# Norm factors with a token to a partition, and gates ahead of attention's end, in a two-layer gated-branch trunk

## The chip, the cores and the metric

The kernel runs on one core of a Trainium2 chip. The metric is the device time of one execution in microseconds. A time is given as the median of several runs; the profile comes from one execution, with its own time.

## The reference, cut to what matters

Two layers of a trunk run over 640 tokens of width 1024: 128 context tokens and 512 latent tokens, with one set of weights. The two groups differ in their modulation vectors, in attention and in the scan's starting state.

```
mod = silu(cond) @ w_mod + b_mod;  shift, scale, gate = split(mod, 3)
h = rmsnorm(x, g_norm) * (1 + scale) + shift
(a_u, a_v, b_r, b_k, b_v, b_wd, b_ad, c_q, c_k, c_v, d_p, z, mg) = split(h @ w_in)
y_a = chunk_mix(a_u, a_v)      # a_u * (128x128 mix of a_v in each chunk + b_s)
y_b = rwkv7_mix(...)           # scan forward and backward, group norm, bonus
y_c = attention(c_q, c_k, c_v) # windows of 128, cached keys and values, sink
y_d = pool_mix(d_p)            # means over 2, 4, 8, 16 tokens minus the token, a small product
ys = stack(y_a, y_b, y_c, y_d) * silu(z)
merged = sum_n sigmoid(mg_n) * (ys_n @ w_up_n)
x = x + gate * (merged @ w_o)
```

After layer 2 a last RMSNorm gives the outputs. rmsnorm divides each token by the root of its mean square over the 1024 features; the factor is one number for each token. Keys, values and the context's last scan states are outputs too.

## The kernel before, in words

Activations lie with features on the partitions and tokens along the free axis: 1024 features are eight tiles (KT) of 128, and the 640 tokens are two halves (b = 0, 1) of HF = 320. Large products are made from three: both operands are split into a high and a low part (`hi`, `lo` for activations, `whi`, `wlo` for weights; ScalarE makes the high part, VectorE the low one), and hi-whi, lo-whi and hi-wlo are added in PSUM. A weight tile of w_in (one entry of ORDER, in two pieces of four blocks) needs 48 products with 320 columns for both halves. All matrix products are issued from line 331, transposes from 335, all work of VectorE, ScalarE and GpSimd from 290, and all loads and stores from 327 on SP's queue, so rows are told apart by their tiles.

PSUM has four banks `m` for these products, two `x` for side work, and one each of `c` and `o`.

The instruction order is made when the kernel is built, by a small planner (`Clock`). There is a main stream (`layer`), which goes through ORDER and the merges, and there are side jobs (modulation, norm, attention, scan, pooling, chunk mixing, modulation rows), each with a priority. A side job that is ready by the planner's estimate goes ahead of the main stream, which fills the rest. A `yield "name"` waits in the planner until that job is marked done; a bare `yield` gives others a turn; `VQ` asks that VectorE's queue be nearly empty. On the chip each engine works through its own instructions in the order that came out, and waits for its operands.

The places that the change touches:

- `rstd_of` makes the norm's factor. `nacc` holds sums of squares (128 feature rows x 320 tokens). A product with a constant matrix of 1/1024 sums over partitions and puts the mean of each token on all 128 partitions; ScalarE takes the square root and VectorE the reciprocal of all 128x320. It runs for both halves at the start (`program`), at the layers' border (`normed`, where the last square tile comes in as `more`) and at the end (`fin`).
- `modulation` makes layer 0's shift and scale: eight jobs, one for each feature tile, each with a load of 1 MB, a `partial` (eight products with `sc`), a copy (`vn`) and two small products with the constant `sel`. The norm's tile k waits for job k. `modulation_rows` makes the other modulation vectors on VectorE from 32 loads of `wt` and a broadcast silu of the conditions (`sil`), one dot product (`junk`) per row and group.
- `gated` multiplies a branch by silu(z): tanh on ScalarE, two multiplications on VectorE, then the split into `ysh` and `ysl`. For attention (z20, z21) it first makes both products, then waits for attention's end (`{L}at`), with both tiles held in the four `m` banks.
- `attention` goes through ten blocks of 128 queries: scores in two parts with masks and maxima on VectorE (tile `kbt`), exponentials on ScalarE, transposes, and the product with the values.
- `pool_mix` copies the product of p0 or p1 into a padded buffer in the tile xm1 and spawns the pooling job; `chunk_v` and `chunk_u` do the chunk mixing of the a branch in the tile xm0. Attention's tables lie in xm1 before, and the merge's sums `mg` take both tiles after.
- `merge` goes through eight feature tiles of a branch: 48 products for the gate mg, 12 for w_up.

The end of `layer`, which orders these:

```python
        g2 = yield from gated(None, f"{L}at")
        ...
        for ft in range(2):
            yield from pool_mix(ft, buf, yd)
            yield from chunk_v(ft, tm, bs, ya)
        yield from chunk_u(ya)
        for ft in range(2):
            yield f"{L}pool{ft}"
        yield from merge(0, g2, mhl)
```

## Time and profile before

| | |
|---|---|
| median of three runs | 1417.62 us (1411.64 to 1418.31) |
| the profiled execution | 1418.08 us, span 1416.0 us |
| TensorE matmul busy | 1358.9 us, 96% of the span |
| VectorE, ScalarE, GpSimd busy | 944.7, 566.8, 50.8 us |
| loaded and stored | 132.59 MB, 94 GB/s in the mean |
| mean granted TensorE clock | 0.991 |

Busy times of engines overlap, so they don't add up to the span. A busy TensorE isn't one at its peak, since matmuls are pipelined and their ends are modelled. PE is TensorE's products, PEld its weight loads, DVE VectorE, ACT ScalarE, POOL GpSimd, SPq SP's queue. A span is the time from the first to the last instruction; the execution's own time is some 2 us longer. The granted clock is a share of TensorE's upper level, 2.4 GHz; its other level is 1.2 GHz.

### The profile page before, as it was taken

How to read it: one execution, taken by the hardware profiler on the slowest of the kernel's cores; microseconds unless marked ns; L12 is line 12 of the kernel's file. 1: busy time of each engine (PE TensorE's matmuls, PEld its weight loads, DVE VectorE, ACT ScalarE, POOL GpSimd, SP SyncE). 2: the span in 40 equal slices, each digit the busy share in tenths (PEclk: the TensorE clock that was granted, in tenths of full speed). 3: DMA queues.
4: the chain of work that ended last, by engine and by line, in shares of the span. 5: the costliest groups of instructions: out<-in, count | busy, mean ns of one | idle time of the engine just before them, and what ended most of it. 6: DMA issues, size and time to landing. Idle time of an engine off the chain costs nothing.

```text
span 1416.0 us, 27587 instructions
## 1 busy us (share of the span) xinstructions
PE 1358.9 (96%) x11274; PEld 1256.8 (89%) x11274; DVE 944.7 (67%) x2096; ACT 566.8 (40%) x1252; POOL 50.8 (4%) x43
## 2 busy tenths in 40 slices
PE   6899988999999999999999999999999999999996
PEld 3788878988999988999988888998799999899996
DVE  6666677755876756656887677795466585464476
ACT  5446522235533233324454655223345233232363
POOL 0000010000000000000001000100000000000001
PEclk9999999999999999999999999999999999999998
DMA  9411214421224412562313111424122323144111
GB/s 369 147 53 61 63 40 120 105 82 56 88 65 112 119 55 75 196 234 62 105 61 112 54 46 39 121 79 118 42 59 69 90 81 89 37 128 173 28 38 75
DMA packets 86503, 132.59 MB, mean 94 GB/s; under 512 B 44745, under 2 KB 46153, under 8 KB 84457
## 3 DMA queue, kind: packets, MB, share of 16 engines
q1 hardware_dynamic: 86376, 130.84, 30.1%
q8 instruction: 88, 1.44, 0.4%
q14 instruction: 39, 0.31, 0.1%
HBM read 120.46 MB, written 10.35 MB: 92 GB/s over the span
## 4 chain that ended last, share of the span: by engine, by line
PE 81%; DVE 10%; ACT 4%; issue 2%; DMA 2%; SPq 0%; POOL 0%; DVEq 0%; ACTq 0%; POOLq 0%
PE m L331 63%; PE x L331 10%; PE c L331 4%; PE o L331 2%; DVE wlo L290 2%; DVE t L290 2%; DVE kb L290 2%; ACT whi L290 1%; DMA kb<-ad 1%; PE x L335 1%; DVE nacc L290 1%; PE o L335 1%; DVE lo L290 1%; ACT vn L290 1%; ACT A L290 1%
## 5 line engine op out<-in xcount | busy, mean ns | idle before, releaser
L331 PE MATMUL m<-hi,whi 128*128 128x320 f32 x2064 | 666.7, 323 | 2.9 <-ACT whi L290 1.3
L331 PE MATMUL m<-lo,whi 128*128 128x320 f32 x2064 | 640.8, 310 | 6.0 <-DVE lo L290 5.1
L331 PE MATMUL m<-hi,wlo 128*128 128x320 f32 x2064 | 642.1, 311 | 3.9 <-DVE wlo L290 3.8
L331 PEld LDWEIGHTS m<-hi,whi 128*128 128x128 f32 x2064 | 389.6, 189 | 27.6 <-issue 11.4
L331 PEld LDWEIGHTS m<-lo,whi 128*128 128x128 f32 x2064 | 390.1, 189 | 10.2 <-DVE lo L290 7.1
L331 PEld LDWEIGHTS m<-hi,wlo 128*128 128x128 f32 x2064 | 389.4, 189 | 8.5 <-DVE wlo L290 8.2
L290 ACT CAST whi<-raw 128x640 fp32r<-128x640 f32 (+1 forms) x220 | 148.7, 682 | 296.3 <-PE m L331 270.6
L290 DVE TENSOR_TENSOR wlo<-raw,whi 128x640 fp32r<-128x640 f32 (+1 forms) x220 | 169.2, 772 | 108.6 <-ACT whi L290 105.8
L290 ACT ACTIVATE t<-m 128x320 f32<-128x320 f32 x160 | 68.3, 437 | 88.2 <-PE m L331 88.0
L290 DVE SCALAR_TENSOR_TENSOR t<-t,m 128x320 f32<-128x320 f32 x128 | 61.6, 482 | 58.9 <-PE m L331 43.5
L290 DVE TENSOR_TENSOR kb<-kb 80x31 f32<-80x31 f32 (+15 forms) x248 | 86.1, 347 | 13.0 <-DMA kb<-ad 6.1
L331 PE MATMUL m<-ysh,whi 128*128 128x320 f32 x256 | 84.3, 329 | 1.8 <-DVE t L290 1.6
L290 DVE CUSTOM_DVE_ANT_0 junk<-wt,sil 128x1024 bf16<-128x1024 f32 x64 | 78.4, 1224 | 3.1 <-DMA wt<-wt 3.0
L331 PE MATMUL m<-ysl,whi 128*128 128x320 f32 x256 | 79.6, 311 | 0.0
L331 PE MATMUL m<-ysh,wlo 128*128 128x320 f32 x256 | 79.6, 311 | 0.0
L331 PEld LDWEIGHTS m<-ysh,whi 128*128 128x128 f32 x256 | 48.6, 190 | 5.1 <-DVE t L290 2.1
L290 DVE TENSOR_TENSOR xm<-xm,t 128x320 f32<-128x320 f32 x96 | 48.5, 506 | 3.3
L331 PEld LDWEIGHTS m<-ysl,whi 128*128 128x128 f32 x256 | 48.7, 190 | 0.4
L331 PEld LDWEIGHTS m<-ysh,wlo 128*128 128x128 f32 x256 | 48.6, 190 | 0.0
L290 DVE RECIPROCAL t<-t 128x320 f32<-128x320 f32 x16 | 34.4, 2150 | 19.5 <-ACT t L290 19.5
L290 ACT ACTIVATE vn<-c 64x128 f32<-64x128 f32 x40 | 10.8, 271 | 80.5 <-DVE vn L290 80.5
L290 DVE CUSTOM_DVE_ANT_0 kbt<-x,xm 128x256 f32<-128x256 f32 (+2 forms) x72 | 28.7, 435 | 16.2 <-PE x L331 16.0
(234 smaller groups left out, 1528.4 us busy)
## 6 DMA issues: line engine op xcount, KB each, us to landing
raw<-wb SPq DMA_DIRECT2D x128, 320.0 KB, 3.0
raw<-wa SPq DMA_DIRECT2D x92, 256.0 KB, 2.8
wt<-wt SPq DMA_DIRECT2D x32, 512.0 KB, 3.7
A<-wm SPq DMA_DIRECT2D x4, 1024.0 KB, 9.0
A<-wo SPq DMA_DIRECT2D x8, 512.0 KB, 4.0
xm<-xt SPq DMA_DIRECT2D x4, 640.0 KB
ad<-A SPq DMA_DIRECT2D x8, 320.0 KB, 4.3
qr<-wm SPq DMA_DIRECT2D x2, 1024.0 KB
```

The lines of the kernel that those rows point to most:

```text
L290: return f(out, *a, **k)
L331: PE.matmul(out, lhsT, rhs, start=start, stop=stop)
L335: PE.transpose(out, in_, K("ident"))
```

## The change

- The norm factors. `rstd_thin` puts a token on a partition: each 128 tokens of the sums of squares are the stationary operand, and two columns of the constant 1/1024 the moving one, so the means come out as 128x2 for each of three token blocks. Square root and reciprocal then run on 128x6. `spread` brings the factors back to all partitions: a column of factors, read 128 times over, is the stationary operand, and the identity is the moving one; a copy puts the result where `rs` is read. At the end VectorE reads the factors from PSUM, and GpSimd the copy.
- The start. The first modulation job's products are issued between the first half's means and its spreading, and the job's second part between the second half's.
- The modulation rows. The load of `sil` is issued when the eight jobs are done, its arithmetic 4 us later by the planner's clock; a row waits for VectorE at most six times.
- Attention. A block whose four key blocks fit one bank makes its scores in one part. `pt` is allocated ahead of `yc`.
- The gates. `gates_early` makes silu(z) up to a factor and keeps it in the tile `ysl`; then p0's product follows, and only then the wait for attention's end; `gates_late` multiplies by the branch and splits.
- Pooling. ORDER has p1 after av1; the pooling jobs are spawned before and after the two chunk_v, the loads of `pc` are issued after the late gates, and the wait for both pooling jobs moves into the merge, behind its first w_up products.

```diff
 PAIRS = (HEAD[0:2], HEAD[2:4])
-ORDER = ["wa", "k0", "v0", "r0", "k1", "r1", "v1", "z20", "z21", "p0", "av0", "p1", "av1", "au0", "au1", 0,
+ORDER = ["wa", "k0", "v0", "r0", "k1", "r1", "v1", "z20", "z21", "p0", "av0", "av1", "p1", "au0", "au1", 0,
          "z00", "z01", 1, "z30", "z31", 2, "z10", "z11", 3]
...
         yield
-        if arrival(0) > 0:
-            yield arrival(0)
         nx = partial(0)
...
             nx = None
-            if i + 1 < len(jobs) and arrival(i + 1) <= 0.05:
+            if i and i + 1 < len(jobs) and arrival(i + 1) <= 0.05:
                 nx = partial(i + 1)
...
         mod_tiles(1)
+        yield "mods0"
         sil = S([P, 2, D], "sil")
...
         w = S([P, D], "wt")
-        yield "mods0"
+        yield 4.0
         for g in range(2):
...
             for g in range(2):
-                while ck.free.get("V", 0.0) > ck.t + 0.3:
-                    yield VQ
+                for _ in range(6):
+                    if ck.free.get("V", 0.0) > ck.t + 0.3:
+                        yield VQ
                 V.tensor_tensor_reduce(junk, w, sil[:, g], 1.0, 0.0, ALU.mult, ALU.add,
...
-    def rstd_of(acc, more=None):
+    def rstd_thin(acc, more=None):
+
         ms = X()
-        mm(ms[:, 0:HF], K("mean"), acc, start=True, stop=more is None)
-        if more is not None:
-            mm(ms[:, 0:HF], K("mean"), more, start=False, stop=True)
-        A.activation(acc, ms[:, 0:HF], AF.Sqrt, bias=eps[:, 0:1])
-        V.reciprocal(acc, acc)
-        return acc
+        parts = [acc] if more is None else [acc, more]
+        for i, o in enumerate((0, P, HF - P)):
+            for x in parts:
+                mm(ms[:, 2 * i:2 * i + 2], x[:, o:o + P], K("mean")[:, 0:2], start=i == 0 and x is acc,
+                   stop=i == 2 and x is parts[-1])
+        st = S([P, 6], "rst", 2)
+        A.activation(st, ms[:, 0:6], AF.Sqrt, bias=eps[:, 0:1])
+        V.reciprocal(st, st)
+
+        def spread():
+            bc = X()
+            for i, (o, c) in enumerate(((0, 0), (P, 0), (2 * P, C))):
+                mm(bc[:, o:min(o + P, HF)], st[:, 2 * i:2 * i + 1].to_broadcast([P, P]), K("ident")[:, c:P])
+            A.copy(acc, bc[:, 0:HF])
+            return bc
+
+        return spread
...
         for b in bs:
-            rs[b] = accs[b] if l == 0 else rstd_of(accs[b], more)
+            rs[b] = accs[b]
+            if l:
+                rstd_thin(accs[b], more)()
         for b in bs:
...
-        def gated(y, need=None):
+        def gated(y):
             hi = S([P, 2, T], "ysh", dt=F32R)
             lo = S([P, 2, T], "ysl", dt=F32R)
-            zs = []
-            if need:
-                for ft in range(2):
-                    zs.append((yield from main()))
-                yield need
-                y = inputs["yc"]
             for ft in range(2):
-                z = zs[ft] if need else (yield from main())
+                z = yield from main()
                 for b in range(2):
...
+        def gates_early():
+
+            early = S([P, 2, T], "ysl")
+            for ft in range(2):
+                z = yield from main()
+                for b in range(2):
+                    t = early[:, ft, hs[b]]
+                    A.activation(t, z[b], AF.Tanh, scale=0.5)
+                    V.scalar_tensor_tensor(t, t, 1.0, z[b], ALU.add, ALU.mult)
+            return early
+
+        def gates_late(early, y):
+            ts = []
+            for ft in range(2):
+                for b in range(2):
+                    ts.append(S([P, HF], "t", 4))
+                    V.scalar_tensor_tensor(ts[-1], early[:, ft, hs[b]], 0.5, y[:, ft, hs[b]], ALU.mult, ALU.mult)
+            hi = S([P, 2, T], "ysh", dt=F32R)
+            lo = S([P, 2, T], "ysl", dt=F32R)
+            for i, t in enumerate(ts):
+                o = (slice(None), i // 2, hs[i % 2])
+                A.copy(hi[o], t)
+                V.tensor_tensor(lo[o], t, hi[o], ALU.subtract)
+            return hi, lo
+
         mg = []
...
         def merge(i, yhl, mhl):
-            if i == 0:
-                mg.extend(x_tile(b) for b in range(2))
             rhs_y = [((lambda k, b=b: yhl[0][:, k, hs[b]]), (lambda k, b=b: yhl[1][:, k, hs[b]])) for b in range(2)]
...
                 yield from accum(up, w, 3, 2, rhs_y, 0, True, True)
+                if i == 0 and dt == 0:
+                    for ft in range(2):
+                        yield f"{L}pool{ft}"
+                    mg.extend(x_tile(b) for b in range(2))
                 for b, g in enumerate(gs):
...
-        def pool_mix(ft, buf, yd):
+        def pool_mix(ft, buf, yd, o):
             pw = prm("pw").rearrange("p (f c) -> p f c", f=2)
-            o = yield from main()
-            if ft:
-                yield f"{L}pool0"
             xp, s2, s4 = (buf[:, i * W:(i + 1) * W] for i in range(3))
...
             yield f"{L}cv"
+            pt = S([P, 2 * T], "y", 2)
             yc = inputs["yc"] = S([P, 2, T], "y", 2)
-            pt = S([P, 2 * T], "y", 2)
             vt = inputs["cv"]
...
                     rs = [slice(0, 64), slice(64, 128)]
-                    px = [X(), X()]
-                    for hh, r in enumerate(rs):
-                        mm(px[hh][:, 0:nl], q2[ft][r, qs], kr[r, lo * P:lo * P + nl])
-                    for hh in range(2):
-                        V.tensor_tensor_reduce(pr[:, hh, 0:nl], px[hh][:, 0:nl], am[:, off:off + nl], 1.0,
-                                               -3.0e38, ALU.add, ALU.max, mp[:, 0, hh:hh + 1])
+                    parts = [[(kr, lo * P, nl)]]
                     if qb:
-                        yield
-                        m = 384 if qb < 4 else 256
-                        px = [X(), X()]
-                        for hh, r in enumerate(rs):
-                            mm(px[hh][:, 0:256], q2[ft][r, qs], kc[r, :])
-                        if qb < 4:
+                        more = [(kc, 0, 256)] + ([(kr, (qb + 1) * P, P)] if qb < 4 else [])
+                        if len(blocks) <= 4:
+                            parts[0] += more
+                        else:
+                            parts.append(more)
+                    at = 0
+                    for j, part in enumerate(parts):
+                        if j:
+                            yield
+                        px, m = [X(), X()], 0
+                        for src, o, w in part:
                             for hh, r in enumerate(rs):
-                                mm(px[hh][:, 256:384], q2[ft][r, qs], kr[r, (qb + 1) * P:(qb + 2) * P])
+                                mm(px[hh][:, m:m + w], q2[ft][r, qs], src[r, o:o + w])
+                            m += w
                         for hh in range(2):
-                            V.tensor_tensor_reduce(pr[:, hh, nl:nl + m], px[hh][:, 0:m], am[:, off + nl:off + nl + m], 1.0,
-                                                   -3.0e38, ALU.add, ALU.max, mp[:, 1, hh:hh + 1])
+                            V.tensor_tensor_reduce(pr[:, hh, at:at + m], px[hh][:, 0:m], am[:, off + at:off + at + m], 1.0,
+                                                   -3.0e38, ALU.add, ALU.max, mp[:, j, hh:hh + 1])
+                        at += m
                     n = len(blocks) * P
                     mx = mp[:, 0]
-                    if qb:
+                    if len(parts) > 1:
                         V.tensor_tensor(mx, mx, mp[:, 1], ALU.max)
...
             ck.mark(L + n)
-        g2 = yield from gated(None, f"{L}at")
-        ya = S([P, 2, T], "y", 2)
-        yd = S([P, 2, T], "y", 2)
-        tm, buf = x_tile(0).rearrange("p k f -> p (k f)"), x_tile(1).rearrange("p k f -> p (k f)")
-        dma(tm[:, 3 * T:3 * T + 512], pc[l][:, 0:512])
-        bs = buf[:, 3 * W:3 * W + 256]
-        dma(bs, pc[l][:, 512:768])
-        dma(buf[:, 3 * W + 256:3 * W + 322], pedge)
+        early = yield from gates_early()
+        p0 = yield from main()
+        yield f"{L}at"
+        buf = x_tile(1).rearrange("p k f -> p (k f)")
         G.memset(buf[:, 0:W], 0.0)
         G.memset(buf[:, W:W + 1], 0.0)
+        bs = buf[:, 3 * W:3 * W + 256]
+        dma(buf[:, 3 * W + 256:3 * W + 322], pedge)
+        yc = inputs["yc"]
+        yd = S([P, 2, T], "y", 2)
+        pool_mix(0, buf, yd, p0)
+        g2 = gates_late(early, yc)
+        ya = S([P, 2, T], "y", 2)
+        tm = x_tile(0).rearrange("p k f -> p (k f)")
+        dma(tm[:, 3 * T:3 * T + 512], pc[l][:, 0:512])
+        dma(bs, pc[l][:, 512:768])
         for ft in range(2):
-            yield from pool_mix(ft, buf, yd)
             yield from chunk_v(ft, tm, bs, ya)
+        p1 = yield from main()
+        yield f"{L}pool0"
+        pool_mix(1, buf, yd, p1)
         yield from chunk_u(ya)
-        for ft in range(2):
-            yield f"{L}pool{ft}"
         yield from merge(0, g2, mhl)
...
             accs.append(acc)
-        for b in range(2):
-            rstd_of(accs[b])
+        spread = rstd_thin(accs[0])
+        next(mod)
+        spread()
+        spread = rstd_thin(accs[1])
+        next(mod)
+        spread()
         split(1)
...
                     def fin(xh=xh, acc=acc, sq=sq, b=b):
-                        rs = rstd_of(acc, sq)
+                        bc = rstd_thin(acc, sq)()
                         A.activation(xh[:, KT - 1], xh[:, KT - 1], AF.Copy, scale=gf[:, KT - 1:KT])
...
                         for k in range(KT):
-                            E = G if k in (1, 3, 6) else V
+                            E, rs = (G, acc) if k in (1, 3, 6) else (V, bc[:, 0:HF])
                             E.tensor_tensor(xh[:, k], xh[:, k], rs, ALU.mult)
...
                                 dma(y_o[:, b, k - 1:k + 1], xh[:, k - 1:k + 1])
```

## Rows read from the trace of the kernel before

**Rows 1.** The page: busy time, share of the span and instructions of each engine.
```profile
PE 1358.9 (96%) x11274; PEld 1256.8 (89%) x11274; DVE 944.7 (67%) x2096; ACT 566.8 (40%) x1252; POOL 50.8 (4%) x43
```

**Rows 2.** TensorE's waits, whole span: us in total, times, longest.
```profile
PE x L331 <- DVE nacc L290: 14.5, 3, 11.1
```

**Rows 3.** Timeline of the start: start us, us, instructions, idle before and releaser.
```profile
4.44 0.47 SPq L327 DMA_DIRECT2D A<-wm  x1
...
14.94 1.43 PE L331 MATMUL x<-nacc,cst 128*128 128x320 f32 x2 [2.45 <-DVE nacc L290]
...
16.30 1.94 PE L331 MATMUL x<-A,sc 128*32 128x256 f32 x16
...
18.73 1.01 PE L331 MATMUL x<-cst,vn 128*128 128x2 f32 x4 [0.49 <-ACT vn L290]
```

**Rows 4.** Timeline, 50 to 58 us.
```profile
51.00 1.28 ACT L290 ACT_TABLE_LOAD   x1
...
54.11 1.22 DVE L290 TENSOR_TENSOR sil<-wt,sil 128x1024 f32<-128x1024 f32 x1
...
57.04 0.41 PE L331 MATMUL m<-lo,whi 128*128 128x320 f32 x1 [3.10 <-DVE lo L290]
```

**Rows 5.** Windows, us: busy time of each engine, granted clock, DMA share, GB/s.
```profile
278.00:288.00 10.00, 10.00 (x226) 9.28 (x225) 4.34 (x9) 3.49 (x8) 0.00 (x0) 1.00 0.70 163
488.00:502.00 14.00, 12.58 (x212) 11.33 (x211) 4.43 (x8) 3.17 (x9) 0.00 (x0) 0.63 0.51 127
...
188.00:192.00 4.00, 4.00 (x16) 3.47 (x15) 2.77 (x7) 1.67 (x5) 0.00 (x0) 0.58 0.01 4
...
57.00:62.00 5.00, 4.96 (x23) 4.97 (x24) 3.33 (x6) 0.94 (x1) 0.00 (x0) 0.66 0.72 217
```

**Rows 6.** Timeline at attention's end, layer 0.
```profile
187.14 1.71 PE L331 MATMUL x<-bon,cst 128*128 128x320 f32 x4 [4.03 <-DVE bon L290]
```

**Rows 7.** TensorE's waits, 200 to 250 us, pooling in layer 0.
```profile
PE x L335 <- DVE xm L290: 1.9, 1, 1.9
PE x L331 <- DVE t L290: 1.8, 1, 1.8
```

**Rows 8.** TensorE's waits, 855 to 935 us, the same places in layer 1.
```profile
PE x L331 <- DVE bon L290: 1.0, 1, 1.0
PE x L335 <- DVE A L290: 0.9, 1, 0.9
```

**Rows 9.** TensorE's waits, 735 to 765 us, the layers' border.
```profile
PE m L331 <- DVE lo L290: 1.5, 2, 1.1
```

**Rows 10.** Timeline of the tail.
```profile
1404.20 0.81 PE L331 MATMUL x<-nacc,cst 128*128 128x320 f32 x2 [1.04 <-DVE nacc L290]
...
1405.58 0.53 ACT L290 ACTIVATE nacc<-x,eps 128x320 f32<-128x320 f32 x1 [1.33 <-PE x L331]
...
1406.14 2.15 DVE L290 RECIPROCAL nacc<-nacc 128x320 f32<-128x320 f32 x1 [2.00 <-ACT nacc L290]
1408.33 4.09 DVE L290 TENSOR_TENSOR xm<-xm,nacc 128x320 f32<-128x320 f32 x5
1408.38 3.29 POOL L290 TENSOR_TENSOR xm<-xm,nacc 128x320 f32<-128x320 f32 x3 [26.75 <-DVE nacc L290]
```

**Rows 11.** Operations by tile (duration ns min/median/max), and the timeline at 46 us.
```profile
L331 PE MATMUL x<-cst,A x80: 269/275/276, 106.9 to 1082.4; 128*128 128x128 f32 x80
...
L290 DVE RECIPROCAL den<-den x20: 166/166/168, 81.1 to 864.4; 128x2 f32<-128x2 f32 x20
...
46.62 0.50 PE L331 MATMUL x<-cst,vn 128*128 128x2 f32 x4
```

**Rows 12.** The page's DMA issues: KB each, us to landing.
```profile
A<-wm SPq DMA_DIRECT2D x4, 1024.0 KB, 9.0
```

**Rows 13.** The chain that ended last, 900 to 925 us.
```profile
912.14 7.04 PE m L331 x48
```

**Rows 14.** SP's queue in the timeline at 175 us.
```profile
175.13 8.39 SPq L327 DMA_DIRECT2D xm<-pc  x2
```

## The prediction

> **What bounds the kernel now.** I read the page first: it gives TensorE 96% of the span [rows 1], so the time can only fall where TensorE stands idle, where it runs at the lower clock, or where its work shrinks. The reader sees 1416.0 - 1358.9 = 57 us of idle time there. Then the list of TensorE's waits: its largest entry is the norm's sums, 14.5 us, of which 11.1 is the wait for the first of them [rows 2]. Next the timeline of the start, where the two means wait for VectorE and two reciprocals stand behind them in VectorE's queue [rows 3]. Then the timeline at 51 to 57 us, where the last tile of the head waits [rows 4], and windows around the waits, which show what the clock adds behind them [rows 5]: (1 - granted clock) x length is time lost. Then the same for attention's end in layer 0 [rows 6, 7], for layer 1 [rows 8], for the border of the layers [rows 9] and for the tail [rows 10]. Everywhere else TensorE is dense, and VectorE, ScalarE and the DMA are covered by it.
>
> **The sum's base.** The profiled execution took 1418.08 us, 2.1 more than its span. It lies 0.5 above the median, 1417.62, and inside the three runs. What this kernel's measurement can tell from no change is about 0.5%, 7 us: below 1410.5 counts as faster, above 1424.7 as slower.
>
> **The start.** Old: both means, then two reciprocals of 2.15 us [rows 10]; the first modulation job (1.94 us of products) starts at 16.30, its two small products end at 18.73 + 1.01 = 19.74 [rows 3]. New: three products with 2 columns give the means, a square root and a reciprocal run on 128x6, and three products with the identity spread the factors. The first job stands between. Prices: two products with 128x2 took 1.01 us at the lower clock level [rows 3] and 0.50 at the higher [rows 11]; products 128x128 from the constants run in halves of 0.275 us at the higher level, pipelined; I take 0.26 for a product there and 0.51 at the lower [rows 11]. A reciprocal on 128x2 took 0.166 us [rows 11]; 128x6 is between that and 2.15, I take 0.17, as the size says. A load of weights that all read one column is not in the trace; below it is bounded by the ordinary product, above by twice that, and I take the ordinary one.
> The first job moves into TensorE's gap before 14.94. Its weights were issued at 4.44 and such a load lands in a median of 9.0 us [rows 3, 12], so at about 13.4; the job would end at 15.3. If they come as late as the old start, 16.30, the job holds up the spreading by 3 us. From about 15.1: spreading 1.3 (two and a half products at 0.51), means of the second half 1.5, the job's small products 1.0, spreading 1.3. This gives 20.2 against 19.74: 0.4 us lost. VectorE's 4.3 us disappear, but TensorE is busy from 16.30 on, so this alone earns nothing.
> What does earn is the order of the modulation rows. Today the table load, two passes of tanh and the products for "sil" reach ScalarE and VectorE at 51.00 to 55.3, ahead of the last tile's factors, and TensorE idles 3.10 us before 57.04 [rows 4]; then 57 to 62 runs at 0.66 of the clock, 1.7 us lost [rows 5]. The new code starts the 1 MB load of sil only when the eight jobs are done, and computes 4 us after that. The load leaves the SP queue's crowded start, where other loads come forward. The same work then meets the copies out of PSUM at the head's end; if it delays them, that is late next. I take 4.8 - 0.4 - 0.4 = 4.0 us gained; bounds 0 and 5.5.
>
> **Attention's end, layer 0.** Today the gates' two products hold all four m banks until attention has ended, so p0's products can't run ahead. TensorE idles 4.03 us behind bon [rows 6] and the clock is at 0.58 for 4 us, 1.7 us lost [rows 5]. New: the gates' tanh and first multiplication go to the ysl tile at once, which frees the banks, and p0 (48 products, 7.04 us [rows 13]) stands ahead of the wait. The number of gate operations is the same. So 7 us of independent products cover the wait for bon. Of 5.7 I take 4.7, because the copies and late gates queue up on VectorE a little later; bounds 1 and 5.7. On SP the two loads of pc held the queue 8.39 us waiting for attention's tile [rows 14]; now pedge waits there first and pc follows behind the late gates. Weight loads queued behind either wait equally long, and TensorE waits for no raw tile there, so this costs nothing; without that cover it could cost those same 8 us.
> **Scores.** Two of five blocks now fill one bank and need one reduction each and no maximum between. That takes work from VectorE and not from TensorE, whose products for main cover it: nothing, either way under 1 us.
> **Pooling, layer 0.** TensorE waits 1.9 and 1.8 us where both pooling tiles and the chunk copies crowd VectorE [rows 7]. With pool 1 after av1, one of the two should go. I take 1.5; bounds -1 and 3.7.
> **Layer 1, the same places.** Waits of 1.0 and 0.9 us [rows 8], no lower clock: I take 1.2; bounds 0 and 1.9.
> **Border of the layers.** Each half's mean was two products of 320 columns, 1.38 us from 1404.20 to the root's start in the tail [rows 10]. New: six thin ones at 0.2 and two and a half at 0.26, 1.85 in all: 0.5 more. And the spreading now waits in TensorE's queue for square root and reciprocal, about 0.5 with nothing issued between. In the trace products behind a waiting product don't pass it [rows 6]. So two halves cost 2.0. In return 2 us of reciprocal leave VectorE ahead of each half's factors; the waits there for lo, 1.5 us [rows 9], and shorter ones should mostly go; with 0.7 for those I take 2.2. Net 0.2; bounds -2 and 1.
> The Trainium skill (TensorE: Matmul & The Clock Gate, Part 2, Step-by-step) says the same: only weight loads are pulled ahead, matmuls keep program order. By it the two halves here and one at the end pay that half microsecond each; if matmuls could pass, the sum would be 1.5 us better. The trace agrees, with its 4.03 us.
> **The end.** First half: 1.0 lost, half of it given back by VectorE, -0.5. Second half: mean at 1404.20, square root, reciprocal 2.15 until 1408.3, then five multiplications in 4.09 us beside GpSimd's three in 3.29 [rows 10]. New: thin products 1.35, root 0.2, reciprocal 0.17, spreading with its latency 0.85: multiplications start at 1406.8 instead of 1408.33. VectorE reads PSUM; GpSimd must wait for a copy of 0.45 us and ends at about 1407.25 + 3.3 = 1410.55, where the last multiplication ended at 1412.42. Gain 1.9 (bounds 1.0 and 2.5), with the first half 1.4.
>
> **Sum.** 4.0 + 4.7 + 1.5 + 1.2 + 0.2 + 1.4 = 13.0. 1418.1 - 13.0 = 1405 us. All lower bounds together would give 1420, all upper ones 1397.
>
> **The rivals.**
> *Gains are taken over.* VectorE has the same work elsewhere, and each wait that goes leaves the next late one, so 4.03 may only pass to wlo or t. Speaking for it: TensorE's remaining waits are short and many, and the sil work is moved, not removed. Then the tail (1.9), half the start (2) and a little of attention's end (1) stay: about 1413 us. Chance 0.22.
> *The clock's low stretch.* The 32x32 products of the inverse run at full clock in the window at 278 but at a mean of 0.63 in 488 to 502, where 14 x 0.37 = 5.2 us are lost, for the same 160 product records [rows 5]. Nothing in the work differs but its place. If the shift by some microseconds ends this stretch, the time is about 1400; if one of the other such places falls into one, 1410. I put 0.12 on the first with the rest as forecast (1396 to 1401); the second lies in my range.
> The Trainium skill (TensorE: Matmul & The Clock Gate, Part 1, What's actually happening) says that the clock's window runs freely and doesn't start with the kernel. By this rule each run may lose or win such a stretch; the trace agrees with the unlike windows, while the three runs, 6.7 us apart, don't show why.
> *Slower: pool 1 becomes the wait.* Its result is now asked for inside the first merge, 22.9 us after p1 (au0 and au1 at 7.04 each, the merge's first tile 60 products, 8.8). In layer 0 VectorE is dense there with the inverse. Against it: TensorE can go on with the next tile's seven microseconds before banks are short. The change turns slower if pool 1 needs over 30 us in both layers and each wait costs over 6.5 us with the lower clock behind it, 13 in all, which uses up the sum; at twice that, 1431. Chance 0.10, half of it beyond no change.
> *Forecast*, 1401 to 1411: 0.56.
>
> **How the numbers follow.** The predicted time is the forecast's. The range 1397 to 1416 leaves the pooling case and part of the first rival above, and little below. Faster by over 0.5%: forecast nearly all and the clock case, 0.68. Within: most of the first rival, the weak end of the forecast and half the pooling case, 0.26. Slower: 0.06.
>
> **What would show it.** The start: a small reciprocal behind the adds, the first job's products ahead of 15 us, the table load behind the last lo, and no gap of 3 us before the head's last products. Attention's end: no wait for bon over 1 us, p0's products in its place, the clock at 1.00. Border: reciprocals of 2.15 gone, a wait of about half a microsecond before each spreading. Tail: the five multiplications start some 2.6 us after the last means, not 4.1 as now [rows 10]. I am wrong if the table load still precedes the head's last tile, if TensorE waits for copies or for pool 1, or if the thin products cost more than 0.25 us each.

## The result, and the profile after

The changed kernel takes 1396.74 us in the median of four runs (1392.85 to 1398.95), the one before 1414.68 (1411.64 to 1418.31); the ratio is 0.9874, with a 95% interval of 0.9847 to 0.9900. Two more measurements of the changed kernel gave 1397.95 and 1396.5 us, ratios 0.9894 and 0.9882. The forecast was 1405, the range 1397 to 1416: right in direction, 8 us too slow, and the time 0.26 us below the range.

The profiled execution took 1396.28 us, 21.8 less than the one before; its span is 1394.2 us. First the page's busy times, which answer to [rows 1]: TensorE is busy 9.3 us less although it has 76 instructions more.

```profile
PE 1349.6 (97%) x11350; PEld 1259.7 (90%) x11350; DVE 925.8 (66%) x2056; ACT 565.3 (41%) x1258; POOL 48.0 (3%) x43
```

TensorE's waits over the whole span answer to [rows 2] (us in total, times, longest). The first wait for the sums stays, as does the one in the tail; the one between them is gone. Four waits for `rst`, ahead of the spreadings at the border and at the end, are new.

```profile
PE x L331 <- DVE nacc L290: 12.0, 2, 10.9
PE x L331 <- ACT A L290: 4.9, 6, 1.4
PE x L331 <- DVE rst L290: 2.5, 4, 0.7
```

The timeline of the start [rows 3]: the first job's products run at 13.30, not 16.30, a reciprocal takes 0.18 us, and the job's small products end at 17.83 in place of 19.74.

```profile
10.87 1.44 PE L331 MATMUL x<-cst,nacc 128*128 128x2 f32 x6 [10.87 <-DVE nacc L290]
...
13.30 1.93 PE L331 MATMUL x<-A,sc 128*32 128x256 f32 x16 [0.98 <-DMA A<-wm]
...
14.62 0.18 DVE L290 RECIPROCAL rst<-rst 128x6 f32<-128x6 f32 x1
15.16 1.36 PEld L331 LDWEIGHTS x<-cst,rst 128*128 128x128 f32 x6 [0.81 <-DVE rst L290]
...
17.22 0.61 PE L331 MATMUL x<-cst,vn 128*128 128x2 f32 x4
```

The head's end [rows 4]: the table load still stands at 50.09, but the arithmetic on `sil` comes behind the last tile's low parts, which now end at 51.6 (six in 2.19 us). The wait of 3.10 us is gone; the weights' high part (1.22 us) and a copy (1.44) are late instead.

```profile
47.15 0.42 PE L331 MATMUL m<-hi,whi 128*128 128x320 f32 x1 [1.22 <-ACT whi L290]
...
49.39 2.19 DVE L290 SCALAR_TENSOR_TENSOR lo<-t,shift,hi 128x128 fp32r<-128x128 f32 x6
50.09 1.28 ACT L290 ACT_TABLE_LOAD   x1
...
55.85 1.23 DVE L290 TENSOR_TENSOR sil<-wt,sil 128x1024 f32<-128x1024 f32 x1
...
59.57 0.41 PE L331 MATMUL m<-hi,whi 128*128 128x320 f32 x1 [1.44 <-ACT xm L290]
```

Attention's end in layer 0 [rows 6]: the products with `bon` start without a wait. The windows behind them answer to those of [rows 5]: the granted clock, third figure from the end, is 1.00 in both.

```profile
183.66 1.24 PE L331 MATMUL x<-bon,cst 128*128 128x320 f32 x4
```
```profile
188.00:192.00 4.00, 4.00 (x37) 3.69 (x36) 3.90 (x10) 3.01 (x8) 0.00 (x0) 1.00 0.04 15
488.00:502.00 14.00, 13.07 (x282) 11.69 (x283) 7.12 (x17) 4.00 (x11) 0.00 (x0) 1.00 0.54 142
```

TensorE's waits at 200 to 250 us [rows 7] and at 855 to 935 [rows 8]:

```profile
PE x L335 <- DVE A L290: 0.5, 1, 0.5
PE x L331 <- DVE t L290: 0.5, 1, 0.5
```
```profile
PE x L331 <- DVE t L290: 1.2, 1, 1.2
PE x L335 <- DVE A L290: 1.0, 1, 1.0
```

The first half's factor at the end shows what a spreading costs: the last of six thin products, a wait, the spreading, and then the products' pace.

```profile
1352.51 0.36 PE L331 MATMUL x<-cst,t 128*128 128x2 f32 x2
1353.45 0.88 PE L331 MATMUL x<-cst,rst 128*128 128x128 f32 x6 [0.58 <-DVE rst L290]
1354.14 0.39 PE L331 MATMUL m<-hi,whi 128*128 128x320 f32 x1
...
1354.91 0.47 PE L331 MATMUL m<-lo,whi 128*128 128x320 f32 x1
```

From 1354.66, 1.2 us after the end of the wait, a product takes 0.46 to 0.47 us in place of 0.31: the lower clock (0.58 at 1354 to 1358 us). The tail [rows 10]:

```profile
1383.45 0.35 PE L331 MATMUL x<-cst,nacc 128*128 128x2 f32 x2 [1.13 <-DVE nacc L290]
...
1385.25 0.19 DVE L290 RECIPROCAL rst<-rst 128x6 f32<-128x6 f32 x1 [1.95 <-ACT rst L290]
1385.59 1.52 PE L331 MATMUL x<-cst,rst 128*128 128x128 f32 x6 [0.67 <-DVE rst L290]
...
1387.60 2.08 DVE L290 TENSOR_TENSOR xm<-xm,x 128x320 f32<-128x320 f32 x5 [2.16 <-ACT nacc L290]
1387.65 2.50 POOL L290 TENSOR_TENSOR xm<-xm,nacc 128x320 f32<-128x320 f32 x3 [29.78 <-ACT nacc L290]
```

In the tail the clock is at the lower level too, 0.50 at 1386 to 1387 us, while the spreading runs: six records take 1.52 us there and 0.88 at 1353.45.

Where the time went is read from one landmark, the residual updates of the first half (operations by tile; the first is layer 0's, the last layer 1's): the kernel before, a second execution of it (below), and the kernel after.

```profile
L290 DVE SCALAR_TENSOR_TENSOR kbt<-m,gt,kbt x32: 346/380/414, 669.9 to 1372.7; 128x128 f32<-128x128 f32 x16, 128x192 f32<-128x192 f32 x16
```
```profile
L290 DVE SCALAR_TENSOR_TENSOR kbt<-m,gt,kbt x32: 346/380/414, 664.1 to 1366.9; 128x128 f32<-128x128 f32 x16, 128x192 f32<-128x192 f32 x16
```
```profile
L290 DVE SCALAR_TENSOR_TENSOR kbt<-m,gt,kbt x32: 349/380/411, 650.1 to 1350.2; 128x128 f32<-128x128 f32 x16, 128x192 f32<-128x192 f32 x16
```

With the second half's last update (1403.2, 1397.4 and 1382.4 us) and the spans (1416.0, 1410.2, 1394.2):

| stretch | forecast | against the first profile | against the second |
|---|---|---|---|
| start to layer 0's first update | 10.2 | 19.8 | 14.0 |
| border and layer 1 | 1.4 | 2.7 | 2.7 |
| first half's end, to the last update | -0.5 | -1.7 | -1.7 |
| tail | 1.9 | 1.0 | 1.0 |
| sum | 13.0 | 21.8 | 16.0 |

### The profile page after: what moved, and what is told of

Same layout as the page of the kernel before. It is cut to its first block, busy times and chain, and to the rows that moved or that the text cites. A ratio compares the mean times of both kernels' runs of the same rounds, so it can differ in the third digit from the quotient of the medians.

```text
span 1394.2 us, 27698 instructions
## 1 busy us (share of the span) xinstructions
PE 1349.6 (97%) x11350; PEld 1259.7 (90%) x11350; DVE 925.8 (66%) x2056; ACT 565.3 (41%) x1258; POOL 48.0 (3%) x43
## 5 line engine op out<-in xcount | busy, mean ns | idle before, releaser
L331 PEld LDWEIGHTS m<-hi,whi 128*128 128x128 f32 x2064 | 389.9, 189 | 25.3 <-issue 10.2
L290 ACT ACTIVATE t<-m 128x320 f32<-128x320 f32 x152 | 64.2, 434 | 87.3 <-PE m L331 87.1
L290 DVE TENSOR_TENSOR kb<-kb 80x31 f32<-80x31 f32 (+15 forms) x248 | 86.2, 348 | 10.2 <-DMA kb<-ad 3.5
L290 DVE SCALAR_TENSOR_TENSOR t<-t,m 128x320 f32<-128x320 f32 x120 | 57.7, 481 | 47.0 <-PE m L331 38.0
L290 DVE TENSOR_TENSOR A<-x,cst 128x512 f32<-128x512 f32 x40 | 25.7, 684 | 20.6 <-PE x L331 20.6
```

What stands on the lines that cost most here:

```text
L290: return f(out, *a, **k)
L331: PE.matmul(out, lhsT, rhs, start=start, stop=stop)
```

## The experiments

The theories at first: A, the gain is the sum of waits that separate parts remove, somewhat undersized; B, a good part is low stretches of the clock (stretches at the lower level) that fall elsewhere; C, the gates carry it alone. A diff is against the changed kernel where nothing else is said, and a part is "undone" when the kernel has its old form again.

**Four undone parts.** `u_rows`: early `sil`, no limit to a row's waits.

```diff
-        yield 4.0
+        yield "mods0"
...
-                for _ in range(6):
-                    if ck.free.get("V", 0.0) > ck.t + 0.3:
-                        yield VQ
+                while ck.free.get("V", 0.0) > ck.t + 0.3:
+                    yield VQ
```

> The changed kernel with the modulation rows as before: sil is loaded early, its arithmetic starts as soon as the eight jobs are done, and a row waits for VectorE without a limit. Theory A (the gain is the sum of TensorE's waits that separate parts removed, each worth some more than the list of waits shows): the 3.1 us wait ahead of the head's last tile is back, with low clock or a lengthened product behind it, so 3.5 to 5 us are lost: 1400 to 1402 us against 1396.7. Theory B (a good part of the gain is the clock's low stretches, which fall elsewhere by chance): the wait may come back, but the time goes by where low stretches fall; the time lies anywhere from 1395 to 1403 and the difference of the traces is in stretches of lower granted clock. Theory C (only the gates with the order around them carry the gain): within 1.5 us of 1396.7.

`u_norm`: `rstd_of` in all three places.

```diff
-        spread = rstd_thin(accs[0])
-        next(mod)
-        spread()
...
+            rstd_of(accs[b])
```

> The changed kernel with the old norm factors in all three places (means on all partitions, root and reciprocal on 128x320) and the old order of the first modulation job. Theory A: the start changes by 0.4 us at most, the border gets its 2.15 us reciprocals and short waits back but loses four waits of about 0.6 us, the tail loses 1.0 to 1.9 us: 1397.5 to 1400 us. Theory B: anywhere from 1395 to 1403, with the difference in low stretches. Theory C: within 1.5 us of 1396.7.

`u_scores`: always two parts.

```diff
-                        if len(blocks) <= 4:
+                        if False:
```

> The changed kernel with attention's scores always in two parts, as before. Theory A: VectorE gets some 20 reductions and maxima per layer back, TensorE's waits stay as they are: 1396 to 1398 us. Theory B: 1395 to 1403. Theory C: within 1.5 us of 1396.7.

`u_gates`: ORDER, `gated`, `pool_mix` and the waits at the layer's end as before.

```diff
-        early = yield from gates_early()
-        p0 = yield from main()
-        yield f"{L}at"
...
+        g2 = yield from gated(None, f"{L}at")
```

> The changed kernel with the old gates, the old order of p1 and av1, and the old pooling and merge waits. Theory A: the 4.0 us wait for bon and the two pooling waits of 1.8 and 1.9 us come back in layer 0, 1 to 2 us in layer 1, with the lower clock behind bon: 7 to 11 us lost, 1404 to 1408 us. Theory B: the waits come back, but a low stretch or two more or less in the scan decide; 1398 to 1412. Theory C: nearly the whole gain is gone, 1411 to 1415 us.

Measured: 1413.41, 1402.79, 1402.16 and 1415.4 us. Against the changed kernel's 1396.74 that is 16.7, 6.0, 5.4 and 18.7 us lost: 46.8 together for a change that brought 17.9. All four undone together are the kernel before, so the prices do not add; `u_rows` and `u_gates` alone are as slow as the kernel before beside them (1412.9 us; ratios 1.0002 and 1.0015). A and C fall as stated. B's range held the norm and the scores and missed the other two, and low stretches are not what those two lost by: the mean clock in their profiles is 0.996, and 0.992 in the changed kernel's. In `u_rows` layer 0's first update comes at 657.5 us, for 650.1, and then TensorE waits 9.46 us for `hi` at the border, a wait that neither the kernel before nor the one after has.

**The two halves of the rows' part, the gates alone, and the changed kernel again.** `u_sil` and `u_cap` are the two hunks of `u_rows`, one each; `o_gates` is the changed kernel with `u_rows`, `u_norm` and `u_scores` at once, so the kernel before with the gates alone.

> The changed kernel once more, unaltered, beside the next three on one chip. Chance theory (a good part of the gain is low stretches of the clock that fall elsewhere): the profile has its low stretches in other places than the first one (713 to 716, 1007 to 1011, 1354 to 1357 us), and the median is several us off 1396.7. Waits theory (the gain is waits removed): the same gaps, median 1394 to 1399 us.

> The changed kernel with sil alone loaded and computed early again; the limit of six waits for a modulation row stays. The undoing of both lost 16.7 us: some 6 us up to the end of the head and 11 us at the layers' border, where the second layer's rows came too late. Theory I (the limit is what brings the rows ahead of the border): only the head's 4 to 6 us are lost, 1401 to 1403 us. Theory II (the early sil moves the rows): the border's wait for hi is back too, 1409 to 1414 us.

> The changed kernel with the limit of six waits removed alone: a modulation row waits for VectorE's queue without a limit; sil stays late. Theory I: TensorE waits 8 to 10 us for hi at the layers' border, since the second layer's rows come too late: 1405 to 1409 us. Theory II: the rows come in time, 1396 to 1399 us.

> The kernel before with the gates alone: gates in two steps, p0 ahead of the wait, p1 behind av1, the pooling waits in the merge; norm factors, rows and scores as before. Undoing this part lost 18.7 us, more than the whole change brought. If prices of parts simply add up: it brings nearly everything, 1395 to 1399 us. If the parts hang together through the planner's order, so that what one of them frees is lost again without the others: it brings the 6 to 8 us of layer 0's attention end and pooling and little else, 1403 to 1410 us, with a long wait for the modulation rows at the border, as in the run without the rows' part.

Measured: 1397.95, 1399.94, 1414.53 and 1409.99 us (the last a ratio of 0.9979 to before, 0.9961 to 0.9997). The late `sil` is worth 2.0 us by this run, less than both theories had; the limit 16.6, more than theory I had (1405 to 1409 us); and the gates alone 1.4, inside the range for parts that hang together. The unaltered kernel came out in the waits theory's range, with low stretches at the first profile's three places (at 715, 1009 and 1357 us) and at one more (681). The timeline of `u_cap` shows the chain: VectorE makes the last row of `shift` at 730.55, the norm's tile follows, and TensorE gets its high part at 731.91.

```profile
728.01 1.23 DVE L290 CUSTOM_DVE_ANT_0 junk<-wt,sil 128x1024 bf16<-128x1024 f32 x1 [3.29 <-DMA wt<-wt]
729.28 1.22 DVE L290 CUSTOM_DVE_ANT_0 junk<-wt,sil 128x1024 bf16<-128x1024 f32 x1
730.55 0.23 DVE L290 TENSOR_SCALAR shift<-mv,pa 128x2 f32<-128x2 f32 x1
730.69 0.68 DVE L290 SCALAR_TENSOR_TENSOR t<-kbt,gsc,nacc 128x128 f32<-128x128 f32 x2
...
731.91 0.64 PE L331 MATMUL m<-hi,whi 128*128 128x320 f32 x1 [15.71 <-ACT hi L290]
```

In `o_gates` the same wait is 11.24 us, with the row at 727.1; in the kernel before the row was made at 702.6 and nothing waited.

**The limit without the rest, with the gates, and a second profile of before.** The hunk of `u_cap`, turned round, in the kernel before (`o_cap`) and in `o_gates` (`o_gates_cap`).

> The kernel before, unaltered, for a second profile of it. Chance theory: the stretch of lower clock at 488 to 502 us, 5.2 us of the first profile, belongs to that execution alone; a profile that comes out near 1411 us lacks it and one near 1418 us has it or another of that size, with the same waits in both. Waits theory: the stretch is there whenever this kernel runs, and executions differ by something else.

> The kernel before with the limit alone: a modulation row waits for VectorE's queue six times at most. In the changed kernel this line is worth 16.6 us. If the limit only prevents a stall that the other parts bring (the second layer's rows late at the border, 15.7 us there in the run without it), it brings nothing here, where that stall is not: 1409 to 1414 us. If it is a gain of its own, near 1396 us.

> The kernel before with the gates and the limit of six, nothing else of the change. The gates alone gained 13 us up to the border in their profile and lost 11.2 us there, waiting for hi. If the limit removes just that stall, the two together bring 1398 to 1401 us, though they bring little each alone. If the stall comes from the gates' own work on VectorE, the time stays at 1407 to 1411 us.

Measured: 1412.31 (one run), 1416.16 and 1405.33 us. The limit alone loses 2.2 us, a little slower than the range expected (ratio 1.0022, 1.0004 to 1.0041), the gates alone gain 1.4, and both together 8.6 (0.9935, 0.9916 to 0.9954), less than expected but far more than the two apart. The wait for `hi` is gone in the last. The limit is thus no gain of its own: it holds off a stall that the other parts bring.

The second profile of the kernel before keeps the waits (3.10 for `lo`, 4.03 for `bon`) and is 5.8 us shorter. The window at 488 has a clock of 0.76, not 0.63; with the limit alone, and no other part of the change, it has 1.00:

```profile
184.68 1.97 PE L331 MATMUL x<-bon,cst 128*128 128x320 f32 x3 [4.03 <-DVE bon L290]
```
```profile
488.00:502.00 14.00, 13.75 (x210) 12.06 (x206) 8.00 (x19) 5.07 (x18) 0.00 (x0) 0.76 0.30 92
```
```profile
488.00:502.00 14.00, 13.59 (x287) 12.10 (x286) 7.26 (x18) 4.53 (x14) 0.00 (x0) 1.00 0.57 145
```

The products of 24 to 36 us show the other part: medians of 0.468 us in the first profile's rows, 0.309 in the second's. Neither theory holds as it stood: the stretch is there again, but shorter, and it is not in the changed kernel's three profiles (1.00 in each). So theory B holds for the base of the forecast and for this one stretch, not for most of the change.

**How early the rows must be, and whether an edit that moves nothing costs.** `range(6)` becomes `range(12)` and `range(3)`; `p_yield8` has `yield 8.0` for `yield 4.0`; `u_border` is the border's part of `u_norm`.

> The changed kernel with a limit of twelve waits in place of six. With six the second layer's last scale row is done at 638.6 us, without a limit at 724.4, behind the need for it. If the limit works through the time of that row: it is done later than 638.6, and as long as it is ahead of about 680 us nothing is lost at the border, 1396 to 1399 us; if it comes behind, the wait for hi at the border is as long as it is late. If the rows' place among VectorE's other work matters by itself, a loss of several us without any wait at the border.

> The changed kernel with a limit of three waits. If the limit only has to bring the second layer's scale rows ahead of the border, three is as good as six, with the last row earlier than 638.6 us: 1395 to 1399 us. If rows that press in early cost, because VectorE is then late for TensorE's next products: 1400 to 1406 us with new short waits between 80 and 640 us.

> The changed kernel with the computing of sil 8 us behind the eight jobs by the planner's clock instead of 4: the same work, moved by 4 us once. If small moves of the order by themselves cost or give some us anywhere later (in the second layer's attention above all), as the undone norm and scores make it look: off by 3 us or more from 1397.3, either way. If the losses seen there were the work of those parts: within 1.5 us of 1397.3.

> The changed kernel with the old norm factor at the layers' border alone; start and end stay new. All three places undone lost 4.8 us, of which the traces show 1 at the end and about 5 in the second layer's attention, none at the border. If VectorE's two reciprocals at the border push that attention back: 1401 to 1403 us, with the wait for bon of 2.7 us there. If the loss came from the order that the start's edit moved: 1396 to 1399 us.

Measured: 1409.92, 1396.03, 1402.97 and 1403.19 us. The rows of `shift` with a limit of three, of six and of twelve (operations by tile; the last start is the last row), and TensorE's wait at the border with twelve:

```profile
L290 DVE TENSOR_SCALAR shift<-mv,pa x8: 219/222/224, 318.8 to 621.3; 128x2 f32<-128x2 f32 x8
```
```profile
L290 DVE TENSOR_SCALAR shift<-mv,pa x8: 215/222/228, 391.2 to 663.6; 128x2 f32<-128x2 f32 x8
```
```profile
L290 DVE TENSOR_SCALAR shift<-mv,pa x8: 220/223/228, 415.8 to 721.3; 128x2 f32<-128x2 f32 x8
```
```profile
PE m L331 <- ACT hi L290: 9.6, 1, 9.6
```

Rows at 621 or 664 us: no wait. At 721: 9.6 us, at 730: 15.7. So the loss goes with the time of these rows, and it is more than the wait: twelve lost 12.9 us in all, with the clock at 0.50 from 716 to 726 us. The expectation had named the scale rows; they are ahead in time at twelve (682.0), and it is the shift rows that come last.

The neutral move of 4 us lost 5.9 us against 1397.1, the mean of the changed kernel's three medians (1400.15 to 1403.69, where sixteen runs of the changed kernel lie at 1392.85 to 1398.95): a wait of 2.17 us behind the scan at 388 us and one of 1.4 for `rst` at the border are new. `u_border` has the wait for `bon` in layer 1, as the expectation had it if the reciprocals push attention back:

```profile
PE x L331 <- DVE bon L290: 2.7, 1, 2.7
PE x L331 <- DVE t L290: 1.7, 1, 1.7
```

But its loss, 6.1 us, is about the neutral move's. Whether the 5 to 6 us of the norm and of the scores are their work or the order that they shift is not told apart here. The same holds for every difference in this section that is no larger than the neutral move's: the late `sil`, the gates alone, the limit alone.

**Products between means and spreading.** `imp_yield`, at the border, and likewise for the first half at the end; `imp_both` adds the limit of three.

```diff
-                rstd_thin(accs[b], more)()
+                spread = rstd_thin(accs[b], more)
+                yield 0.9
+                spread()
```

> The changed kernel with 0.9 us of the planner's time between the thin means and the spreading, at the border and for the first half at the end, so that the main stream's products stand between. The three waits for rst of 0.6 to 0.7 us should go, 1.9 us in all, and each a little more than the list of waits shows: 1394 to 1396 us. If the planner's order elsewhere moves by this edit as much as by the others, anything from 1393 to 1402 us, with the waits for rst gone all the same.

> The changed kernel unaltered, as the base on this chip for the next run: 1395 to 1399 us as in its two earlier measurements. If the lower clock behind the waits for rst comes with the wait, at least two of the three stretches (behind 680, 713 and 1355 us) are below 0.8 again; if it is chance, they lie anywhere.

> The changed kernel with the main stream's products between the thin means and the spreading, and a limit of three waits for a modulation row. If the waits for rst and the lower clock behind them are a loss that can be had back: 1392 to 1395 us, 2 to 4 us below the changed kernel on this chip. If the order gives the gain back elsewhere, as a neutral move of 4 us cost 5.6: within 2 us of it, or above.

Measured: 1396.9, 1396.5 and 1391.43 us. The unaltered kernel's third profile has the lower clock behind one of its three waits (0.57 at 1356 to 1360 us; 1.00 at 680 to 684 and 714 to 718), where the expectation asked for two: the waits are there each time, the lower clock isn't. The three waits for `rst` are gone in `imp_yield` and `imp_both`, and the first half's end, from its last update to the second half's, takes 30.0 us in both, 32.2 in the changed kernel's three profiles and 30.5 in the kernel before. `imp_yield` alone shows no difference (ratio 0.9871, 0.9851 to 0.9891): a wait of 2.47 us for a pooling tile at 914 us is new. `imp_both` is 5.1 us below the changed kernel on the same chip, and no run of the one (1390.66 to 1394.5) reaches the other's (1394.93 to 1398.06): the fastest kernel here, 0.9852 of before (0.9827 to 0.9876). But 5.1 us is less than the neutral move's 5.9, and 5.0 of the 6.1 us between the two profiles lie ahead of layer 0's first update (653.3 and 648.3 us), where no product was put between. So the gain at the first half's end is shown, and what brought the rest is not.

## Why the prediction was wrong

**The step that failed is the sum's base, and with it the rival of the low stretch.** The sum was taken from 1418.08, "0.5 above the median" of three runs. It lies near the upper end of what this kernel takes: five later series of the kernel before, 11 to 23 executions each, have medians of 1411.43 to 1413.97 us, and the four runs beside the result 1414.68. So 3 to 7 of the 8.3 us by which the forecast was too slow are in the base. Side by side, by medians, the change gained 17.9, 13.5 and 16.3 us in its three measurements, where 13.0 were forecast. The second profile shows what such a difference is made of. It took 1412.31 with the same instructions and nearly the same waits, 5.8 us less: 2.5 of it by the products with `bon` (184.68 for 187.14 us), the rest by layer 0's first update, with the lower clock shorter at 24 to 36 and at 488 to 502 us. From 1412.3 the same 13.0 us give 1399.

Against that profile the change gained 16.0 us, 3 more than forecast. That is, in size, the stretch at 488 itself. The sum let it stand; the rival put its end at 5.2 us, gave it a chance of 0.12, and named 1396 to 1401. In the second profile it is worth 14 x 0.24 = 3.4 us, and in the changed kernel's three profiles it is not there. `o_cap` lacks it as well, with none of the gates, so, as far as one profile can show, a shift of the order is enough to end it; what starts it stays open. In `o_cap` other low stretches took its place: the mean clock is 0.989.

The main products (`hi` or `lo` with `whi` or `wlo`) are 6240 in every profile, so their count marks the same amount of main work in each kernel. Stage by stage, in us gained by the profile after:

| stretch | forecast | against the first profile | against the second |
|---|---|---|---|
| start to the 480th main product | 4.0 | 4.5 | 2.1 |
| 480th to 1800th (attention's end, pooling) | 6.2 | 8.1 | 7.1 |
| 1800th to layer 0's first update (the stretch at 488) | 0 | 7.2 | 4.8 |

**Terms of the right size.** Attention's end and pooling in layer 0, 4.7 + 1.5: bon's 4.03 us and the pooling waits went, the clock is at 1.00 behind them, and waits of 0.5 and 0.5 stay. The stretch from the 480th to the 1800th main product takes 319.3 us in the second profile of before, 312.1 to 313.7 in the changed kernel's three, 318.8 in `u_gates` and 313.5 in `o_gates`: 5 to 7 us by the gates, where 6.2 were forecast. The border, 0.2: from the first update to the norm's last tile (745.6 and 730.7 us) it takes 81.5 us in the second profile of before and 80.6 after, 0.9 less; with the old factor there, in `u_border`, 82.1 (650.6 to 732.7). The half microsecond ahead of each spreading is 0.58 to 0.68. No product passed a waiting one: the main products stand still until the spreading is through, at 1354.14.

**Terms mis-sized.** *The start, 4.0:* the gap of 3.10 went as described, but waits of 1.22 and 1.44 us for high parts and copies took part of it, as "late next" had it. Against the second profile of before, the changed kernel's three profiles are ahead by 2.1, 0.8 and 0.2 us at the 480th main product. *The tail, 1.9:* 1.0. The multiplications started 4.15 us after the first means, as late as before (4.13), not 2.6: six thin means took 1.5, and the spreading, at the lower clock, 1.52 in place of the 0.85 that was taken and that it took at the first half's end (0.88). What was gained came from the multiplications, 2.08 us for 4.09. *The first half at the end, -0.5:* -1.7. The price of each spreading left out the lower clock that can follow it. In windows right behind the spreadings of the changed kernel's second profile the clock is 0.62, 0.63 and 0.60:

```profile
680.00:684.00 4.00, 3.88 (x18) 3.89 (x19) 2.17 (x8) 1.80 (x4) 0.00 (x0) 0.62 0.82 253
...
714.00:718.00 4.00, 4.00 (x21) 4.00 (x21) 1.61 (x3) 1.79 (x4) 0.00 (x0) 0.63 0.88 283
...
1356.00:1360.00 4.00, 4.00 (x21) 4.00 (x20) 1.90 (x3) 2.01 (x4) 2.99 (x3) 0.60 0.01 4
```

In the changed kernel's three profiles six of nine such places have it, and in all twelve profiles with a spreading right behind its thin means 16 of 34 have a stretch at 0.50 that begins within 3 us of the wait's end; of the six places in `imp_yield` and `imp_both`, where products stand between, none is below 1.00. The first half's end takes 32.2 us in the seven profiles that have such a stretch there and 30.6 to 31.2 in the five that don't: against 30.5 before, so without it the -0.5 would have been about right. The Trainium skill (TensorE: Matmul & The Clock Gate, Part 1, A second HAM failure mode: psum-queue depth-cycling) tells of a kernel in which short idles between groups of products come often enough that the clock goes back and forth; the trace agrees in that short idles can be enough, but here one idle of 0.6 us behind thin products was followed by the lower clock in about half of the places. *Layer 1, 1.2:* 1.8 (2.7 less the border's 0.9). Here `u_gates` lost most: from the first to the last update it takes 712.1 us (657.2 to 1369.3), the changed kernel 700.1, 12 us, with waits for `t` of 4.4 and 2.4 us that the kernel before did not have and a clock of 0.57 at 865 to 869 and 902 to 910 us: the price of one part undone is a price in that order.

**A term that was missing.** "A row waits for VectorE at most six times" got no number. It is 16.6 us in the changed kernel, not as a gain, but as the stall that the gates would otherwise bring at the border (11.2 us of wait in `o_gates`). The sum could come near only because that line was in the diff. The scores' "nothing" can't be judged (5.4 undone, within the neutral move's 5.9).

**Rivals.** *Gains are taken over* fell in the sum, though it is just what happens without the limit: 1414.5. *Slower, pool 1 becomes the wait:* fell; its waits for `t` are 0.5 and 1.2 us. *The clock's low stretch* came, partly in the base and partly as a gain of 3.4 us; that the time, 1396.74, lies in its 1396 to 1401 is in part luck, since the start fell short and layer 1 gave more. The range's lower end is a slip of the sum as well: all upper bounds together are 19.8 us, which gives 1398, not 1397.

## What to carry to other kernels

Take the base from many executions, and profile a second one before subtracting anything from the first: here one program's two profiles lay 5.8 us apart, more than the largest term. In a kernel whose order a planner writes, undo parts singly and in pairs before pricing them, set their prices beside that of an edit that only moves the order (5.9 us here), and look at the last start of every side job that a later stage needs: rows that kept TensorE waiting for 9.6 us cost 12.9, and rows made another 42 us earlier gained nothing. A short dependent chain on TensorE (thin product, other engines, product) should have independent products put into its middle, because its wait can bring the lower clock with it. Here that gave 2.2 us at the place itself, and nothing in the whole kernel's time as long as it stood alone.

## What was not expected of the hardware

At the start, 24 to 36 us, the first profile's row of granted clock says 1.00 while its 128x320 products take 0.468 us until 34 us and 0.309 afterwards: the pace of the lower clock without its record.

VectorE's five multiplications of 128x320 took 4.09 us beside GpSimd's with both operands in SBUF [rows 10], and 2.08 with one of them in PSUM; a single addition of that shape with both in SBUF and no GpSimd beside it took 0.48 (in the tail after, at 1382.82 us); GpSimd's three fell from 3.29 to 2.50 without an edit of theirs but the copy. The Trainium skill (VectorE: DVE Perf Modes, Two Vector instructions with no wait between them) names a second SBUF read interface that VectorE needs for two SBUF inputs and shares with GpSimd; the two rows agree with that, and no run here tells the interface from another cause.

A spreading of two 128-column products and one of 64, all reading one column as weights, took 0.88 us at the higher level (six records), and the next main product starts 0.69 us after the first of them: the unknown price of such a load lay at its lower bound.
